# Keeping the outputs of layer 0's last two experts on chip, with the gates applied by slot

## The chip, the cores and the metric

The kernel runs on one core of a Trainium2 chip. The metric is the device time of one execution in microseconds (us). Three executions of the kernel before gave 885.44, 887.4 and 891.0 us, a median of 887.4. TensorE is called PE, VectorE DVE, ScalarE ACT, GpSimd POOL and SyncE SP. Each engine takes its instructions in a fixed order, and each of SP, ACT and POOL also issues DMAs from that same order.

## The reference

The reference is a two-layer transformer block over 256 tokens and 256 context tokens of width 1024. In each layer the two streams pass a modulated RMS norm, three kinds of attention and an output product; then each token is routed to two of 16 experts:

```python
w = w / jnp.sum(w, axis=-1, keepdims=True)
gates = jnp.sum(jax.nn.one_hot(expert_idx, N_EXPERTS) * w[..., None], axis=1)
for e in range(N_EXPERTS):
    hid = jax.nn.silu(t @ w_gate[e]) * (t @ w_up[e])
    out = out + gates[:, e:e + 1] * (hid @ w_down[e])
...
x = x + g2 * moe_ffn(hx, ...)
```

All is float32. Layer 0 routes all 512 tokens, that is four tiles of 128 (two of the context, two of x). Layer 1 needs only x, and its experts run in another way ("paired"), which the change touches in names alone.

## The kernel before, in words

A float32 product is made of three: each operand is split into a rounded part and the rest (`whi`, `wlo` of a weight; `xh`, `xl` or `Xh`, `Xl` of the tokens), and `mm3` issues hi by hi, lo by hi, hi by lo. ACT casts the hi part (L234), DVE subtracts for the lo part (L235).

**Layer 0's routing, then its experts.** `Route.lists` (L1840 and on) ends the routing. One-hot rows `ohs` (slot by token, for the first and the second choice) times token numbers gave `ips`, from which `idx` says for each expert which token stands in each of its 128 slots. `rows` says for each token in which row of the table `yrows` its two expert outputs will stand, and `gates` with what weights. `experts` then loops over 16 experts: an indirect DMA gathers an expert's tokens from `h2row` (`xg`); PE transposes them; ACT and DVE split them; `first` makes gate and up products from split weights (`produce` splits one half of a weight at a time, up to LEAD ahead); `hidden`, `turn` and `second` make y, the expert's output by slot. `write` copies y from PSUM on ACT (L211) and writes it by a DMA from ACT's queue to `yrows` in DRAM (L1095). All this is issued in the order in which it is written (`manual_schedule`).

**The seam between the layers** is `next_in`, also in written order. `combine` issues eight indirect gathers on POOL (L1393): per tile of tokens two, `yc`, one for each choice. `sum_pairs` has the steps of a tile: `one` (ACT: first choice times gate, L1405), `both` (DVE: plus second choice times gate, L1408), `times` (by g2, L1411, on DVE for tile 0 and on POOL for the others), `add` (into the tokens, L1414). `tokens_in` has the norm and the modulation: `square` (ACT, L226), `root` (DVE `ms` and POOL `rstd`, L219 and L221), `scale` (`xn`, DVE, L655), `turn` (eight PE transposes, L193), `modulate` (`xf`, four pieces on ACT, L686, and four on DVE, L684), `high` (`Xh`, ACT, L690) and `low` (`Xl`, DVE, L694). `half(t, h)` then issues 12 products 128x512 of tile t with half of the weight columns `w_in` (L205 to L207). In a turn of the loop PE gets the transposes of tile t-1, `half(t-2, 1)` and `half(t-1, 0)`.

A `Ring` hands out places for weights on their way in, and issues the next load when a place is given back.

## Time and profile before

| | |
|---|---|
| median of three executions | 887.4 us |
| profiled execution | 888.22 us, of which the span of instructions 886.3 |
| mean granted TensorE clock | 0.95 of 2.4 GHz |
| PE busy | 784.3 us (88% of the span) |
| DVE busy | 582.4 us (66%) |
| ACT busy | 447.6 us (50%) |
| POOL busy | 222.2 us (25%) |
| chain that ended last | PE 66%, DVE 16%, DMA 8%, ACT 3%, issue 3%, POOL 2% |

Matmuls are pipelined, so an entry's duration is longer than the spacing of two in a row; where a rate matters, the starts of the first and the last of a row are compared. The granted clock has two levels, 1.2 and 2.4 GHz, printed as 0.50 and 1.00; a window that holds both shows a mean of them. The loop of the experts runs from about 342 to 500 us, the seam from 500 to 553.

### The profile page before, as it was taken

How to read it: one execution, taken by the hardware profiler on the slowest of the kernel's cores; microseconds unless marked ns; L12 is line 12 of the kernel's file. 1: busy time of each engine (PE TensorE's matmuls, PEld its weight loads, DVE VectorE, ACT ScalarE, POOL GpSimd, SP SyncE). 2: the span in 40 equal slices, each digit the busy share in tenths (PEclk: the TensorE clock that was granted, in tenths of full speed). 3: DMA queues.
4: the chain of work that ended last, by engine and by line, in shares of the span. 5: the costliest groups of instructions: out<-in, count | busy, mean ns of one | idle time of the engine just before them, and what ended most of it. 6: DMA issues, size and time to landing. Idle time of an engine off the chain costs nothing.

```text
span 886.3 us, 12972 instructions
## 1 busy us (share of the span) xinstructions
PE 784.3 (88%) x4731; PEld 576.3 (65%) x4731; DVE 582.4 (66%) x1200; ACT 447.6 (50%) x861; POOL 222.2 (25%) x258
## 2 busy tenths in 40 slices
PE   4899999889989977999999549998899797999984
PEld 0578878445557746999999438887555565656541
DVE  1577673879863798899999586697667566221226
ACT  2454442667773416888888546462466543111112
POOL 2000101556320133443342472100423101000200
PEclk9999999999999988999999859999899997999987
DMA  9952221667879337899993757342188955999981
GB/s 319 344 185 96 95 96 48 247 270 284 275 214 376 121 148 263 306 388 401 400 408 156 249 195 292 128 158 95 51 331 215 340 186 215 350 423 422 419 333 51
DMA packets 54505, 219.18 MB, mean 247 GB/s; under 512 B 10299, under 2 KB 10299, under 8 KB 36640
## 3 DMA queue, kind: packets, MB, share of 16 engines
q1 hardware_dynamic: 40816, 182.34, 55.0%
q0 software_dynamic: 8736, 24.92, 7.9%
q10 hardware_dynamic: 4880, 11.00, 3.2%
q8 instruction: 39, 0.64, 0.3%
q14 instruction: 34, 0.28, 0.1%
HBM read 207.09 MB, written 16.84 MB: 253 GB/s over the span
## 4 chain that ended last, share of the span: by engine, by line
PE 66%; DVE 16%; DMA 8%; ACT 3%; issue 3%; POOL 2%; SPq 0%; ACTq 0%; POOLq 0%; DVEq 0%
PE mm L207 7%; PE mm L206 7%; PE mm L205 7%; PE tp L193 6%; PE gu L1189 6%; PE ada L459 4%; PE gu L207 4%; PE gu L205 3%; PE gu L206 3%; DMA wraw<-in_w_up 3%; PE sc L1466 3%; PE w L1245 3%; DVE wlo L235 2%; PE w L1154 2%; DVE nm L1480 2%
## 5 line engine op out<-in xcount | busy, mean ns | idle before, releaser
L235 DVE TENSOR_TENSOR wlo<-wraw,whi 128x1024 fp32r<-128x1024 f32 x136 | 186.1, 1392 | 43.0 <-ACT whi L234 40.5
L234 ACT CAST whi<-wraw 128x1024 fp32r<-128x1024 f32 x152 | 152.8, 1050 | 57.7 <-PE mm L207 35.5
L205 PE MATMUL mm<-whi,Xh 128*128 128x512 f32 x288 | 116.3, 405 | 5.1 <-ACT Xh L690 4.7
L206 PE MATMUL mm<-wlo,Xh 128*128 128x512 f32 x288 | 115.3, 400 | 0.5 <-DVE wlo L235 0.5
L207 PE MATMUL mm<-whi,Xl 128*128 128x512 f32 x288 | 115.0, 399 | 0.5 <-DVE Xl L694 0.5
L221 POOL TENSOR_TENSOR rstd<-ms,cst 128x1 f32<-128x1 f32 (+2 forms) x34 | 29.4, 864 | 272.1 <-DVE ms L219 263.2
L1493 ACT ACTIVATE e<-sc,nm 128x512 f32<-128x512 f32 (+1 forms) x96 | 58.4, 613 | 42.4 <-DVE nm L1486 22.6
L207 PE MATMUL gu<-whi,xl 128*128 128x256 f32 x256 | 74.3, 290 | 0.0
L205 PE MATMUL gu<-whi,xh 128*128 128x256 f32 x256 | 74.2, 290 | 0.0
L206 PE MATMUL gu<-wlo,xh 128*128 128x256 f32 x256 | 72.7, 284 | 0.0
L1189 PE MATMUL gu<-wraw,xq 128*64 128x256 f32 x512 | 64.4, 396 | 3.7 <-DMA wraw<-in_w_up 3.7
L205 PEld LDWEIGHTS mm<-whi,Xh 128*128 128x128 f32 x288 | 55.1, 191 | 18.7 <-ACT Xh L690 6.2
L207 PEld LDWEIGHTS mm<-whi,Xl 128*128 128x128 f32 x288 | 55.0, 191 | 13.9 <-DVE Xl L694 1.5
L206 PEld LDWEIGHTS mm<-wlo,Xh 128*128 128x128 f32 x288 | 55.1, 191 | 12.8 <-DVE wlo L235 1.2
L235 POOL TENSOR_TENSOR wlo<-wraw,whi 128x1024 fp32r<-128x1024 f32 x16 | 42.7, 2672 | 81.1 <-ACT whi L234 50.3
L1189 PEld LDWEIGHTS gu<-wraw,xq 128*64 128x64 f32 x512 | 37.9, 142 | 24.1 <-DMA wraw<-in_w_up 4.2
L193 PEld LDWEIGHTS tp<-ident,e 128*128 128x128 f32 x240 | 26.1, 142 | 40.8 <-issue 21.1
L1480 DVE TENSOR_REDUCE nm<-sc 128x1 f32<-128x512 f32 x64 | 41.2, 684 | 16.5 <-PE sc L1466 11.6
L207 PEld LDWEIGHTS gu<-whi,xl 128*128 128x128 f32 x256 | 49.3, 193 | 1.1 <-DVE xl L1050 0.4
L205 PEld LDWEIGHTS gu<-whi,xh 128*128 128x128 f32 x256 | 49.6, 194 | 0.3 <-ACT xh L1049 0.3
L206 PEld LDWEIGHTS gu<-wlo,xh 128*128 128x128 f32 x256 | 49.5, 193 | 0.0
L193 PE MATMUL tp<-ident,e 128*128 128x128 f32 x240 | 37.8, 286 | 8.4 <-DVE e L1534 3.9
(348 smaller groups left out, 1625.4 us busy)
## 6 DMA issues: line engine op xcount, KB each, us to landing
wraw<-in_w_ada SPq DMA_DIRECT2D x40, 1024.0 KB, 4.9
wraw<-in_w_gate SPq DMA_DIRECT2D x32, 1024.0 KB, 10.1
wraw<-in_w_up SPq DMA_DIRECT2D x32, 1024.0 KB, 11.0
wraw<-in_w_down SPq DMA_DIRECT2D x32, 1024.0 KB, 14.1
wraw<-in_w_in SPq DMA_DIRECT2D x14, 1024.0 KB, 5.2
wraw<-in_w_ada SPq DMA_DIRECT2D x16, 512.0 KB, 8.1
yrows<-y ACTq DMA_DIRECT2D x16, 512.0 KB, 8.1
wraw<-in_w_in POOLq DMA_DIRECT2D x5, 1024.0 KB, 11.9
```

Source lines behind the costliest of these rows:

```text
L193: self.nc.tensor.transpose(out, in_, self.k["ident"][:n, :n])
L205: mm(out, lhsT=xh, rhs=wh, start=start, stop=False)
L206: mm(out, lhsT=xh, rhs=wl, start=False, stop=False)
L207: mm(out, lhsT=xl, rhs=wh, start=False, stop=stop)
L221: nc.gpsimd.tensor_tensor(r, ms, self.k["mhalf"][:, :width], OP.pow)
L234: nc.scalar.copy(h, raw[:, lo:hi])
L235: (engine or nc.vector).tensor_tensor(l, raw[:, lo:hi], h.bitcast(F32), OP.subtract)
L459: nc.tensor.matmul(ps[32 * j:32 * j + 32, :], lhsT=self.silu_c[:, kc, :], rhs=raw[:, 512 * j:512 * j + 512], start=kc == 0, stop=kc == NKC ...
L1189: nc.tensor.matmul(gu[PSLOTS * g:PSLOTS * g + PSLOTS, 256 * b:256 * b + 256], lhsT=xq[q][:, kc, c:c + PSLOTS], rhs=raw[:, kc * 256:kc * 25 ...
L1245: nc.tensor.matmul(y[hf][gs], lhsT=hT[:, c, 0:PSLOTS] if p == NP else hT[:, c, gs], rhs=raw[:, c * D + o * 512:c * D + o * 512 + 512], sta ...
L1480: V.reduce_max(self.nm[:, i:i + 1], self.ps[i], axis=AX.X)
L1493: nc.scalar.activation(self.e[i][:, :self.nkey], self.ps[i], AF.Exp, scale=0.125, bias=self.nm[:, i:i + 1], accum_out=self.z[i])
```

## The change

The outputs of experts 14 and 15 (`LATE_E = 2`) of layer 0 are not written to DRAM. They stay on chip as `ylate`, already times their gates, split in two parts by ACT and DVE. Per tile, products with one-hots `turned` (slot by token, 128x128 for each tile and each of the two experts) take them to their tokens: 32 products 128x512 into PSUM. A token whose choice is expert 14 or 15 gathers a row of zeros instead: the gathers read 14 experts' rows plus one row, which is zeroed at the start of the kernel. So the gathers no longer depend on the last two experts.

The gate is applied where y is copied from PSUM, by slot. For that, `weigh` (in the routing) makes the normalised weights, splits them into three float16 parts, and eight small products with `ohs` bring them to the slots. `one` is gone; `both` is a plain sum; `plus` adds the PSUM banks of the late products. In the seam `times` is always on DVE, all eight pieces of `modulate` are on ACT, and `square(t)` comes behind both halves. Two of the four `w_in` splits, and the place for the ring `rawD`, come later. The bank `ada` of layer 1's projection becomes a fourth `tp` bank.

```diff
-PS_IN = dict(mm=4, ada=1, tp=3)
+PS_IN = (dict(mm=4, ada=1, tp=3), dict(mm=4, tp=4))
...
+            if self.late(0):
+                zeros = self.per.tile([128, 512], F32, tag="modrow", name="zeros")[:, :NKC]
+                nc.gpsimd.memset(zeros, 0.0)
+                z = (NEXP - self.late(0)) * SLOTS
+                nc.gpsimd.dma_start(self.yrows[z:z + 1, :].rearrange("o (p k) -> (o p) k", k=NKC), zeros)
...
-        def modulate(h):
+        def modulate(h, act=False):
...
-                    if b % 2:
+                    if b % 2 and not act:
                         nc.vector.tensor_scalar(xf[b][:, c], tv[:, c], mul, add, OP.mult, OP.add)
                     else:
                         nc.scalar.activation(xf[b][:, c], tv[:, c], AF.Identity, scale=mul, bias=add)
...
-            for name, t in (("one", 0), ("both", 0), ("times", 0), ("one", 1), ("add", 0)):
-                step(sums, t, name)
+            for k in range(self.late(l - 1)):
+                for t in range(2):
+                    step(sums, t, "late", k)
+            for name in ("both", "plus", "times", "add"):
+                step(sums, 0, name)
+            for k in range(self.late(l - 1)):
+                step(sums, 2, "late", k)
             step(ins, 0, "square")
             step(sums, 1, "both")
             step(ins, 0, "root")
-            step(sums, 1, "times", self.nc.gpsimd)
-            step(sums, 2, "one")
+            step(sums, 1, "plus")
             for t in range(1, 6):
                 step(ins, t - 1, "scale")
-                step(sums, t + 1, "both")
-                step(sums, t + 1, "times", self.nc.gpsimd)
-                step(sums, t, "add")
+                if t == 1:
+                    parts.extend(next(split) for _ in range(2))
                 for h in range(2):
                     step(ins, t - 1, "turn", h)
-                    step(ins, t - 1, "modulate", h)
+                    step(ins, t - 1, "modulate", h, True)
+                    step(ins, t - 1, "high", h)
                 half(t - 2, 1)
-                step(ins, t - 1, "high", 0)
-                step(ins, t - 1, "high", 1)
+                step(sums, t, "times")
+                step(sums, t, "add")
                 step(ins, t, "square")
-                step(sums, t + 2, "one")
                 step(ins, t - 1, "low", 0)
+                step(ins, t - 1, "low", 1)
+                if t == 1:
+                    parts.extend(split)
+                    for k in range(self.late(l - 1)):
+                        step(sums, 3, "late", k)
+                    self.ring.open(self.rawD, "rawD", RAW["D"], 2)
+                step(sums, t + 1, "both")
                 step(ins, t, "root")
+                step(sums, t + 1, "plus")
                 if t == 1:
                     self.ring.until(2, self.nc.gpsimd)
-                step(ins, t - 1, "low", 1)
                 half(t - 1, 0)
...
-            w[u] = self.split(t, s * 1024, s * 1024 + 1024, nc.gpsimd if name == "w_down" and s else None)
+            w[u] = self.split(t, s * 1024, s * 1024 + 1024, nc.gpsimd if name == "w_down" and s and n < N - 1 else None)
...
+            if k >= 0:
+                y = self.rawD.tile([128, 2, D], F32R, tag=f"rawD{k}", name="ylate")
...
+                    nc.scalar.activation(y[:, 0, o], ys[n][hf], AF.Copy, scale=gate)
+                    nc.vector.scalar_tensor_tensor(y[:, 1, o], ys[n][hf], gate, y[:, 0, o].bitcast(F32), OP.mult,
+                                                   OP.subtract)
+                return
+            y = mo.tile([128, D], F32, tag="y", name="y", bufs=2)
...
-                self.copy(y[:, hf * 512:hf * 512 + 512], ys[n][hf], True)
+                nc.scalar.activation(y[:, hf * 512:hf * 512 + 512], ys[n][hf], AF.Copy, scale=gate)
...
-            nc.vector.scalar_tensor_tensor(y0, y1, self.gates[:, 1, i:i + 1], y0, OP.mult, OP.add)
+            nc.vector.tensor_tensor(y0, y0, y1, OP.add)
+
+        def late(k):
+            if k == 0:
+                bs.extend(self.bank("tp") for _ in range(2))
+            for hf in range(2):
+                for part in range(2):
+                    nc.tensor.matmul(bs[hf], lhsT=self.turned[k][:, i * 128:i * 128 + 128],
+                                     rhs=self.ylate[k][:, part, hf * 512:hf * 512 + 512],
+                                     start=k == part == 0, stop=part == 1 and k == len(self.ylate) - 1)
+
+        def plus():
+            for hf, b in enumerate(bs):
+                o = slice(hf * 512, hf * 512 + 512)
+                nc.vector.tensor_tensor(y0[:, o], y0[:, o], b, OP.add)
...
+            if ps == 0:
+                self.weigh()
+            gate = m.rt.tile([128, 16], F32, tag=f"gate{ps}", name="gate")
+            for i in range(T):
+                for w in range(2):
+                    self.nc.tensor.matmul(ips[:, 64:112], lhsT=self.ohs[i][:, w],
+                                          rhs=self.gv[:, w, i].rearrange("p a e -> p (a e)"),
+                                          start=i == w == 0, stop=i == T - 1 and w == 1)
...
+        for k in range(late):
+            m.turned.append(m.per.tile([128, 512], F32R, tag=("modrow", "brow")[k], name="turned"))
+            for i in range(T):
+                V.tensor_scalar(m.turned[k][:, i * 128:i * 128 + 128], cst[:, C_IOTA:C_IOTA + 128],
+                                own[:, i, k:k + 1], None, OP.is_equal)
```

What this does to the order on the engines, at three places. First DVE at the end of layer 0's routing, before the change (`wlo` is the first expert's weights, `xl` its tokens):

```order
L1854 TENSOR_SCALAR idx<-ips 128x16
L1860 TENSOR_TENSOR picke<-oh,cst 128x128
L1866 TENSOR_TENSOR pickg<-oh,score 128x128
L1862 TENSOR_REDUCE e<-picke 128x8
L1867 TENSOR_REDUCE gates<-pickg 128x8
L1863 SCALAR_TENSOR_TENSOR rows<-e,first 128x8
L1868 TENSOR_TENSOR gsum<-gates 128x4
L1869 RECIPROCAL gsum<-gsum 128x4
L1870 TENSOR_TENSOR gates<-gates,gsum 128x8
L235 TENSOR_TENSOR wlo<-wraw,whi 128x1024 x4
L1050 TENSOR_TENSOR xl<-tp,xh 128x512 x2
```

DVE at the same place after the change, from the row that now comes ahead of `idx`; these eight rows hold nine operations up to the first part of `gv`:

```order
L1945 TENSOR_TENSOR pickg<-oh,score 128x128
L1906 TENSOR_SCALAR idx<-ips 128x16
L1946 TENSOR_REDUCE g<-pickg 128x8
L1947 TENSOR_TENSOR g<-g 128x4
L1948 RECIPROCAL g<-g 128x4
L1949 TENSOR_SCALAR g<-g 128x4
L1951 TENSOR_TENSOR pickg<-pickg,g 128x64 x2
L1952 CAST gv<-pickg 128x8x16
```

The weights are now made first, to be split. DVE again, five small operations further on, from `gate`, which takes the result of PE's small products, to the first expert's tokens:

```order
L1915 TENSOR_REDUCE gate<-ips 128x16
L1923 SCALAR_TENSOR_TENSOR e<-e,pos 128x8
L1928 TENSOR_SCALAR g<-ips 128x2
L1916 TENSOR_SCALAR gate<-gate 128x16
L1924 TENSOR_SCALAR rows<-e 128x8
L1928 TENSOR_SCALAR g<-ips 128x2 x3
L1932 TENSOR_SCALAR turned<-cst,g 128x128 x8
L239 TENSOR_TENSOR wlo<-wraw,whi 128x1024 x4
L1076 TENSOR_TENSOR xl<-tp,xh 128x512 x2
```

In all, 22 small operations (`idx` among them) and eight one-hots 128x128 now stand ahead of the first `wlo`, where there were nine small ones from `idx` on.

Second, DVE in the seam, before the change, from the last `wlo` to the first tile's `Xl`:

```order
L235 TENSOR_TENSOR wlo<-wraw,whi 128x1024 x4
L1408 SCALAR_TENSOR_TENSOR yc<-yc,gates 128x1024
L1411 TENSOR_TENSOR yc<-yc,wraw 128x1024
L1414 TENSOR_TENSOR xc<-xc,yc 128x1024
L1408 SCALAR_TENSOR_TENSOR yc<-yc,gates 128x1024
L219 TENSOR_SCALAR ms<-nss 128x1
L655 TENSOR_SCALAR xn<-xc,rstd 128x1024
L1408 SCALAR_TENSOR_TENSOR yc<-yc,gates 128x1024
L1414 TENSOR_TENSOR xc<-xc,yc 128x1024
L684 TENSOR_SCALAR xf<-tp,sc_2522,sh_2521 128x128 x4
L694 TENSOR_TENSOR Xl<-xf,Xh 128x4x128
```

And after it, to the first `Xl` again:

```order
L1125 SCALAR_TENSOR_TENSOR ylate<-y,gate,ylate 128x512 x4
L1443 TENSOR_TENSOR yc<-yc 128x1024
L1457 TENSOR_TENSOR yc<-yc,tp 128x512 x2
L1460 TENSOR_TENSOR yc<-yc,wraw 128x1024
L1463 TENSOR_TENSOR xc<-xc,yc 128x1024
L1443 TENSOR_TENSOR yc<-yc 128x1024
L223 TENSOR_SCALAR ms<-nss 128x1
L1457 TENSOR_TENSOR yc<-yc,tp 128x512 x2
L671 TENSOR_SCALAR xn<-xc,rstd 128x1024
L239 TENSOR_TENSOR wlo<-wraw,whi 128x1024 x2
L1460 TENSOR_TENSOR yc<-yc,wraw 128x1024
L1463 TENSOR_TENSOR xc<-xc,yc 128x1024
L710 TENSOR_TENSOR Xl<-xf,Xh 128x4x128 x2
```

The first tile's sum no longer follows `wlo`; the sum takes `plus` from PSUM (`yc<-yc,tp`), `times` (`yc<-yc,wraw`) of each tile is now here, and the pieces `xf` have left.

Third, ACT in the seam, before the change, from the last y copy to the second tile's square:

```order
L211 COPY y<-y 128x512 x2
L1095 DMA yrows<-y 128x1024
L156 DMA wraw<-in_w_in 128x4x512
L234 CAST whi<-wraw 128x1024 x4
L1405 ACTIVATE yc<-yc,gates 128x1024 x2
L226 ACTIVATE xn,nss<-xc 128x1024
L1405 ACTIVATE yc<-yc,gates 128x1024
L686 ACTIVATE xf<-tp,sh_2521,sc_2522 128x128 x4
L690 CAST Xh<-xf 128x4x128 x2
L226 ACTIVATE xn,nss<-xc 128x1024
```

And after it:

```order
L1124 ACTIVATE ylate<-y,gate 128x512 x4
L230 ACTIVATE xn,nss<-xc 128x1024
L238 CAST whi<-wraw 128x1024 x2
L702 ACTIVATE xf<-tp,sh_2524,sc_2525 128x128 x4
L706 CAST Xh<-xf 128x4x128
L702 ACTIVATE xf<-tp,sh_2524,sc_2525 128x128 x4
L706 CAST Xh<-xf 128x4x128
L230 ACTIVATE xn,nss<-xc 128x1024
```

The last DMA to `yrows` and the products by gate are gone; eight pieces `xf` and both `Xh` of a tile now stand between one tile's square and the next one's.

## Rows read from the trace of the kernel before

**Rows 1.** Windows view, core 0: busy us (instructions) per engine, TensorE clock, DMA share, GB/s.

```profile
352.00:499.00 147.00, 146.05 (x1045) 136.47 (x1044) 134.20 (x131) 125.84 (x176) 59.62 (x27) 1.00 0.86 336
```

**Rows 2.** Timeline of DVE, 334 to 343 us: start, duration, instruction [idle before <-releaser].

```profile
333.97 0.48 DVE L1836 TENSOR_SCALAR ohs<-cst,pos 128x128 f16<-128x128 f32 x2
...
334.83 0.28 DVE L1860 TENSOR_TENSOR picke<-oh,cst 128x128 f32<-128x128 f32 x1
...
336.47 4.63 DVE L235 TENSOR_TENSOR wlo<-wraw,whi 128x1024 fp32r<-128x1024 f32 x4
341.56 1.50 DVE L1050 TENSOR_TENSOR xl<-tp,xh 128x512 fp32r<-128x512 f32 x2 [0.46 <-ACT xh L1049]
```

**Rows 3.** Timeline of PE, the same stretch.

```profile
334.31 0.39 PE L1837 MATMUL ips<-val,ohs 128*128 128x16 f16 x2 [0.71 <-DVE ohs L1836]
334.55 3.61 PE L352 MATMUL tp<-mask,ones 128*128 128x256 bf16 x20
340.17 1.55 PE L193 MATMUL tp<-ident,xg 128*128 128x128 f32 x8 [2.00 <-DMA xg<-h2row,idx]
...
342.31 0.58 PE L207 MATMUL gu<-whi,xl 128*128 128x256 f32 x1
```

**Rows 4.** Timeline of PE, layer 0's last y product to the fourth tile of layer 1.

```profile
500.01 0.39 PE L207 MATMUL y<-whi,hl 128*128 128x512 f32 x1
520.51 1.97 PE L193 MATMUL tp<-ident,xn 128*128 128x128 f32 x8 [20.12 <-DVE xn L655]
523.88 0.79 PE L205 MATMUL mm<-whi,Xh 128*128 128x512 f32 x1 [1.40 <-ACT Xh L690]
...
530.04 1.87 PE L193 MATMUL tp<-ident,xn 128*128 128x128 f32 x8
...
537.22 1.03 PE L193 MATMUL tp<-ident,xn 128*128 128x128 f32 x8
...
543.62 1.09 PE L193 MATMUL tp<-ident,xn 128*128 128x128 f32 x8
```

**Rows 5.** Windows view of the seam between the layers.

```profile
526.00:532.00 6.00, 6.00 (x20) 4.88 (x20) 3.69 (x5) 1.68 (x4) 5.96 (x7) 0.52 0.52 164
553.00:573.00 20.00, 19.97 (x92) 16.30 (x91) 14.27 (x38) 8.93 (x21) 2.23 (x2) 1.00 0.28 106
```

**Rows 6.** Timeline of ACT, the end of layer 0.

```profile
488.98 0.33 ACTq L1095 DMA_DIRECT2D yrows<-y  x1
```

**Rows 7.** Timeline of POOL, the same stretch and on.

```profile
491.53 5.99 POOL L235 TENSOR_TENSOR wlo<-wraw,whi 128x1024 fp32r<-128x1024 f32 x2 [7.09 <-ACT whi L234]
504.95 1.00 POOL L1393 DMA_INDIRECT yc<-yrows,rows  x1 [7.43 <-DMA yrows<-y]
...
515.50 0.99 POOL L1393 DMA_INDIRECT yc<-yrows,rows  x1 [0.30 <-issue]
```

**Rows 8.** DMA view, 486 to 540 us: queue, count, KB, median us from issue to landing.

```profile
yrows<-y ACTq DMA_DIRECT2D x3, 512.0 KB, 5.4
...
yc<-yrows,rows POOLq DMA_INDIRECT x8, 5.5
```

**Rows 9.** Timeline of DVE in the seam.

```profile
511.76 1.28 DVE L1408 SCALAR_TENSOR_TENSOR yc<-yc,gates 128x1024 f32<-128x1024 f32 x1 [0.79 <-DMA yc<-yrows,rows]
...
517.62 2.83 DVE L655 TENSOR_SCALAR xn<-xc,rstd 128x1024 f32<-128x1024 f32 x1 [0.69 <-POOL rstd L221]
```

**Rows 10.** Timeline of ACT in the seam.

```profile
515.59 1.06 ACT L226 ACTIVATE xn<-xc 128x1024 f32<-128x1024 f32 x1 [1.54 <-DVE xc L1414]
...
521.67 1.51 ACT L686 ACTIVATE xf<-tp,sh,sc 128x128 f32<-128x128 f32 x4 [3.89 <-PE tp L193]
523.21 0.62 ACT L690 CAST Xh<-xf 128x512 fp32r<-128x512 f32 x1
```

**Rows 11.** Lines of 500 to 552.9 us by form: busy us, mean ns | idle before it.

```profile
L221 POOL TENSOR_TENSOR rstd<-ms,cst 128x1 f32<-128x1 f32 x4 | 3.2, 808 | 9.1 <-DVE ms L219 9.1
...
L655 DVE TENSOR_SCALAR xn<-x,rstd 128x1024 f32<-128x1024 f32 x2 | 1.5, 754 | 0.9 <-POOL rstd L221 0.9
```

90 lines of the change are left out of this document (58 added, 32 removed).

## The prediction

> **What bounds the kernel now.** I began with the shares of busy time by engine and the chain that ended last: PE is on two thirds of that chain, so what counts is where PE stands still or slow. The windows show where it doesn't. In the loop of layer 0's experts PE is busy 146.05 of 147 us at full clock [rows 1], and behind the seam 19.97 of 20 us [rows 5]. In such a stretch a late start is not caught up and an early one is not lost. So the change is worth what it shifts at the two places where PE waits: the start of the loop, and the seam between the layers. PE's timeline and its waits show both: ahead of the loop 2.00 us for the first gather [rows 3], and in the seam 20.12 us until DVE's `xn` lets the first tile's transposes go [rows 4]. The reader is to follow that `xn` back: the sum of tile 0 waits for gathered rows [rows 9], the first gather waited 7.43 us for the last experts' rows to land in DRAM [rows 7], and these could be written only behind the last y product at 500.01 [rows 4].
>
> **The start of the loop (loses).** `wlo` of the first expert now stands behind 22 small DVE operations and eight one-hots, where nine small ones stood. In the old order the eight small ones from `picke` to `wlo` took 336.47 - 334.83 = 1.64 us, 0.2 us each [rows 2]. The new ones up to the split weights `gv` number twelve, at 0.2 us each 2.4 us, from about 334.7 to 337.1. Then PE makes eight small products; two like them took 0.39 us [rows 3], so eight take some 1.5 us, to 338.6. DVE has three operations to do meanwhile, then `gate` and eight small ones wait for PE. These are mostly independent of each other, and I take 0.08 us each, 0.6 in all, since small independent ones overlap (an estimate; at 0.2 it is 1.6). The eight `turned` follow: two `ohs` of the same size took 0.48 us [rows 2], so eight take 1.9. They end at 341.1, and the four `wlo` (4.63 us [rows 2]) at 345.7. Then comes `xl`, 0.75 us for the first half, half of 1.50 [rows 2]. The first product that needs it, at 342.31 before [rows 3], goes at 346.4: **+4.1 us**. The gather of the first tokens, which PE waited for until 340.17 [rows 3], does not hide this: it was ready while DVE was still in `wlo`, and `wlo` with `xl` behind it is last in both orders. PE's 20 warming products (3.61 us [rows 3]) now stand behind the small ones and end near 342, still ahead of `xl`. ACT's casts no longer wait for DVE's `pickg`, which gains nothing. Bounds: if the small ones overlap throughout and `turned` are faster, +2.5; if each costs 0.2 and PE's clock needs longer to come back, +5.6. PE has no slack in the 147 us that follow, so it reaches the seam in full.
>
> **The loop itself (nothing).** The y copy with a gate is the same ACT pass. Two y buffers in place of three: a write lands 5.4 us after its issue [rows 8], within an expert's period (147 us are some 15 experts, 9.8 us each). The last expert's second `wlo` moves from POOL to DVE, one pass of 1.16 us (4.63/4) [rows 2], where PE has products queued. The zeroing of one row lies at the kernel's start on POOL and under the first weight loads; its cover is the wait for those loads, and without it it would cost about one POOL issue, 1 us [rows 7].
>
> **The seam (gains, then gives back).** All on the clock of before; the +4.1 comes on top.
> - *Gathers.* The first one now waits for expert 13's write, issued at 488.98 [rows 6], 5.4 us to landing [rows 8]: 494.4. POOL's `wlo`, two in 5.99 us from 491.53 [rows 7], had its first done by about 494.5. So the gathers go from 494.7 and not from 504.95 [rows 7]; with 1.3 us between issues and 5.5 us to landing [rows 8], tile 0's pair is there at 502 to 503.
> - *Late outputs.* The last y product ends at 500.4 [rows 4]. Two ACT and two DVE passes of 128x512 follow, alternating, 0.62 us each by the `Xh` row [rows 10]: done at 502.4. PE has done expert 14's products by then and needs 1 us for tile 0's last four (128x512 products go at 0.23 us each: 24 of them and 8 transposes lie between 537.22 and 543.62 [rows 4]).
> - *Tile 0.* `both` 502.8 to 504.0 (1.2, a 128x1024 pass as `wlo`), `plus` two halves 1.4, `times` 1.2, `add` 1.2: 507.8. `square` 1.06 [rows 10] with its small ends, to 509.2; `rstd` 0.81 and `xn` 0.75 [rows 11], no longer 2.83 beside POOL's `times` [rows 9]: **transposes at 511**, not 520.51 [rows 4], **9.5 us earlier**.
> - *First product.* Ahead of it PE has tile 3's eight late products, which need banks that come free when all eight `xf` are done: 0.5 + 1.5 + 0.62 + 1.5 us [rows 10] from 512, then 1.8 to 3.4 us for the eight, so about 518; before 523.88 [rows 4]. **Six earlier.**
> - *Tiles 1 to 3.* The period of a tile was PE's work, 543.62 - 537.22 = 6.40 us [rows 4]. Now one chain runs in series from a tile's transposes to the next one's: half the transposes 0.6, four `xf` 1.5, `Xh` 0.62, four `xf` 1.5, `Xh` 0.62 [rows 10], `square` 1.06 and its small ends 0.5, `rstd` 0.81, `xn` 0.75 [rows 11] = about **8 us**. Before, DVE took half of the `xf` at the same time, and the chain stayed under PE's work. The second tile's transposes come at about 523.5 (12 products from 518 at half clock), not 530.04; the third's at 532, not 537.22; the fourth's at 540.5, not 543.62 [rows 4]. Behind the seam PE has no slack [rows 5], so what stands there stays: **-3 us**.
>
> All 32 late products cost 32 x 0.23 = 7.4 us of PE, nearly all in the old gap of 20.12 us; without that cover they would cost just that. Bounds of the seam: -7 if the chain overlaps better than its sum, +5 if the clock stays low (below).
>
> **Sum.** 888.22 + 4.1 - 3 = 889.3 for the profiled execution, which lies 0.8 above the median of the runs shown; against that median 888.5. I say **889**.
>
> **The clock, row against rule.** Before, PE is idle from 500.4 to 520.5 [rows 4] and the clock granted in 526 to 532 is 0.52, so nearly all of that window at 1.2 GHz; it is back at 1.00 from 532 on [rows 5], some 8 us behind the first dense product. I take the same here: half clock up to the second tile, then full. The Trainium skill, "TensorE: Matmul & The Clock Gate", section "HAM oscillation — how this bites in real kernels", says that PE work in bursts with waits between can be throttled again and again, each burst starting cold. No row here shows whether gaps of under 2 us in an 8 us period do that. By the rule the clock would stay low through the tiles, which is the second rival.
>
> **The rivals.**
> 1. *The lead is kept* (chance 0.12). If `xf` and `Xh` of a tile's halves overlap with the transposes and the period stays near 6.4, the 9.5 us come through to 6 or all, and if the start costs only 2.5: 888.2 - 9.5 + 2.5 = 881, at worst 888.2 - 6 + 2.5 = 885. For it: DVE's `xn` at 2.83 [rows 9] was slow beside POOL and POOL is now quiet. Against it: the chain's rows sum to 8 us, and ACT is one engine.
> 2. *The clock stays at 1.2 GHz through the tiles* (0.14; ends slower). PE waits about 1.6 us in each 8 us period. At half clock a tile is 24 x 0.43 + 1.9 = 12.2 us (12 products in about 5.2 of the 6.16 us between 523.88 and 530.04, which hold a wait; transposes 1.87 [rows 4]). Then the tiles start at 523.5, 535.7 and 547.9, the last 4.3 later than 543.62: 888.2 + 4.1 + 4.3 = 896.6. It decides if the second tile's products still run low. For it: low clock was the state there before, until 532 [rows 5]. Against it: PE is denser before the tiles than it was, since 32 late products stand in the old gap.
> 3. *The gathers don't come earlier* (0.12): POOL issues them while DVE is busy 134 of 147 us [rows 1], and the rows land no sooner than the 511.76 at which the first sum could go before [rows 9]. Then the transposes are at 520, and the slower period takes 4.8 us by the fourth tile: 888.2 + 4.1 + 4.8 = 897. For it: POOL's own pass slowed DVE's `xn` from 0.75 to 2.83 [rows 9, 11], so the two do disturb each other. Against it: the old gathers also went beside DVE passes and landed in 5.5 us [rows 8]. The Trainium skill, "SBUF — State Buffer", section "Who interferes with whom", says that a DMA issued from POOL can be starved while DVE holds the port that they share. By that page this rival is how it goes; the trace of before bears it out only so far that one pass was slowed, and no gather landed late there.
>
> **How the numbers follow.** The forecast, a small loss or gain, has 0.62, its own range 885 to 893 by the bounds of the two terms. Rival 1 reaches to 880, rivals 2 and 3 to 898. With a tenth left out on each side the range is 880 to 897. A measurement of this kernel tells 1%, 8.9 us, from no change. Faster by more than that, under 878.5, needs the whole lead and a hidden start: 0.1, more than rival 1 alone gives, for gains in the seam that the rows don't show. Slower, over 896.3: half of rivals 2 and 3 and a little of the forecast, 0.15. Within 1%: 0.75.
>
> **What would show it.** First `xl` product near 346.4; gathers from about 499 (494.7 + 4.1); first transposes of layer 1 at about 515; spacing of the four tiles' transposes about 8 us with PE waiting for `xn` each time; clock 1.00 from about 536. The forecast is wrong if the spacing is 6.4 (rival 1), if clock 0.50 lasts beyond 540 (rival 2), if the first gathered pair lands behind 512 (rival 3), or if the time moved at a place not named here, as in layer 1's weight loads.

## The result, and the profile after

The change took **895.95 us** (median of five runs, 894.08 to 896.15) against 887.4 for the kernel before: a ratio of 1.0083, 95% interval 1.0056 to 1.0110. It is slower by 0.8%, within 1% by these runs, though the interval reaches past 1% and e9 (the same kernel again, below) came out at 1.0129. It lies 7 us above the forecast of 889. The profiled execution took 895.97 us, 7.75 more than that of before. The engines and the chain that ended last, on the page of the profile after (its span is 894.1 us):

```profile
PE 799.9 (89%) x4771; PEld 585.6 (65%) x4771; DVE 589.3 (66%) x1220; ACT 451.1 (50%) x873; POOL 206.2 (23%) x256
PE 65%; DVE 17%; DMA 6%; ACT 5%; issue 3%; POOL 2%; ACTq 0%; SPq 0%; DVEq 0%; POOLq 0%
```

The shares say almost nothing: POOL works 16.0 us less than before, PE 15.6, DVE 6.9 and ACT 3.5 us more. So I cut both traces at PE rows that stand in both kernels and compared the stretches between. Times are us between the starts of two PE rows. The last column is e9, the changed kernel run once more without any edit, which tells what repeats.

| stretch, from one PE row to the next | before | after | differs by | e9 |
|---|---|---|---|---|
| layer 0: first scores of attention to early output products (not changed) | 120.62 | 123.02 | +2.40 | 120.32 |
| on to routing's first `ips` (not changed) | 59.06 | 58.89 | -0.17 | 59.10 |
| `ips` to the first product with `xl` | 8.00 | 13.02 | **+5.02** | 13.00 |
| on to the second expert's first such product | 9.11 | 9.85 | +0.74 | 9.86 |
| on to the last gate and up product | 141.72 | 142.12 | +0.40 | 142.10 |
| on to the last y product | 6.87 | 10.11 | **+3.24** | 10.86 |
| on to the first tile's transposes of `xn` | 20.50 | 10.24 | **-10.26** | 10.48 |
| on to the fourth tile's | 23.11 | 29.97 | **+6.86** | 29.55 |
| on to the scores of layer 1's attention | 82.27 | 84.20 | **+1.93** | 84.23 |
| on to the end | 246.69 | 244.40 | -2.29 | 243.43 |

The first and the last row nearly cancel. The first does not repeat in e9; 1.8 of the last row's 2.29 lie in layer 1's output product, which takes about 27.3 or 28.9 us from run to run and took 29.07 before. What repeats is the middle: start +6.2 (three rows), the loop's end +3.2, the seam -3.4, layer 1's projection +1.9.

**The start.** PE's timeline and DVE's, at the same place as [rows 3] and [rows 2]. Columns: start, duration, instruction [idle before it <- releaser].

```profile
339.51 0.48 PE L1912 MATMUL ips<-gv,ohs 128*128 128x48 f16 x8 [2.71 <-DVE gv L1955]
343.72 1.04 PE L197 MATMUL tp<-ident,xg 128*128 128x128 f32 x8
349.42 0.38 PE L211 MATMUL gu<-whi,xl 128*128 128x256 f32 x1 [3.64 <-DVE xl L1076]
```

```profile
339.16 0.29 DVE L1955 TENSOR_TENSOR gv<-picke,gv 128x128 f16<-128x128 f32 x1
...
340.64 3.56 DVE L1932 TENSOR_SCALAR turned<-cst,g 128x128 fp32r<-128x128 f32 x8
344.12 4.64 DVE L239 TENSOR_TENSOR wlo<-wraw,whi 128x1024 fp32r<-128x1024 f32 x4
348.69 1.27 DVE L1076 TENSOR_TENSOR xl<-tp,xh 128x512 fp32r<-128x512 f32 x2
```

DVE goes without a pause from one row to the next, and PE waits 3.64 us for what DVE makes last, the `xl` behind the four `wlo`. That is the forecast's picture. The eight `turned` took 3.56 us, though, 0.445 each and not 0.24. Ahead of them PE's eight small products took 0.48 us, where I had put down 1.5, and DVE's twelve operations up to `gv` 2.8 instead of 2.4.

**The loop's end and the seam.** DVE, then PE (as [rows 4]).

```profile
496.37 2.34 DVE L239 TENSOR_TENSOR wlo<-wraw,whi 128x1024 fp32r<-128x1024 f32 x2
...
500.83 3.84 DVE L239 TENSOR_TENSOR wlo<-wraw,whi 128x1024 fp32r<-128x1024 f32 x2 [0.65 <-ACT whi L238]
504.60 0.41 DVE L1094 TENSOR_TENSOR hid<-hid,gu 128x256 f32<-128x256 f32 x1
506.01 0.42 DVE L1104 TENSOR_TENSOR hl<-hT,hh 128x256 fp32r<-128x256 f32 x1 [1.01 <-ACT hh L1103]
506.60 1.41 DVE L1125 SCALAR_TENSOR_TENSOR ylate<-y,gate,ylate 128x512 fp32r<-128x512 f32 x2 [0.17 <-ACT ylate L1124]
```

```profile
505.06 0.51 PE L197 MATMUL hT<-ident,hid 128*128 128x128 f32 x2 [0.64 <-DVE hid L1094]
507.41 0.80 PE L209 MATMUL y<-whi,hh 128*128 128x512 f32 x1 [1.84 <-DVE ylate L1125]
...
511.50 0.39 PE L211 MATMUL y<-whi,hl 128*128 128x512 f32 x1
511.73 5.89 PE L1450 MATMUL tp<-ylate,turned 128*128 128x512 f32 x24
521.74 1.97 PE L197 MATMUL tp<-ident,xn 128*128 128x128 f32 x8 [4.12 <-DVE xn L671]
...
526.51 2.93 PE L1450 MATMUL tp<-ylate,turned 128*128 128x512 f32 x6 [0.84 <-ACT xf L702]
529.24 0.63 PE L209 MATMUL mm<-whi,Xh 128*128 128x512 f32 x1
...
534.73 1.10 PE L197 MATMUL tp<-ident,xn 128*128 128x128 f32 x8 [1.68 <-DVE xn L671]
...
543.62 1.09 PE L197 MATMUL tp<-ident,xn 128*128 128x128 f32 x8 [2.17 <-DVE xn L671]
```

The wait of 20.12 us is gone: 5.89 us of it are late products, 4.12 still a wait. In its place there are waits of 1.68 and 2.17 us ahead of the second and third tile, both for `xn`, where [rows 4] have none. And ahead of the last twelve y products PE waits 0.64 us for `hid`, which stands behind two `wlo` on DVE, and 1.84 us for expert 14's `ylate`, which holds the PSUM banks that these products need. The two `wlo` are slow there: 3.84 us beside POOL's `wlo` (499.99 to 502.46, below), where the pair from 496.37 took 2.34.

The clock, in the windows view (busy us per engine with instructions, then granted clock, DMA share, GB/s):

```profile
508.00:513.00 5.00, 5.00 (x18) 4.01 (x17) 1.04 (x3) 1.37 (x2) 2.28 (x3) 0.74 0.98 383
522.00:531.00 9.00, 7.42 (x21) 5.33 (x21) 7.48 (x8) 7.09 (x14) 0.53 (x1) 0.50 0.17 62
531.00:544.00 13.00, 9.14 (x45) 6.99 (x44) 10.97 (x16) 5.21 (x12) 4.99 (x7) 1.00 0.99 361
544.00:548.00 4.00, 4.00 (x16) 3.30 (x15) 2.61 (x3) 3.63 (x10) 0.00 (x0) 0.59 1.03 389
534.73:543.62 8.89, 6.71 (x33) 5.28 (x33) 6.90 (x10) 5.21 (x12) 3.03 (x5) 1.00 0.98 350
543.62:551.71 8.09, 8.09 (x33) 6.57 (x34) 4.59 (x6) 5.21 (x12) 0.55 (x1) 0.79 1.03 385
```

PE ran at half clock behind three of its waits, and at full clock behind the one of 1.68 us. The last two rows are the periods of the second and the third tile, from transposes to transposes. In the first of them PE is busy 6.71 of 8.89 us and waits for `xn`. In the other it doesn't wait at all: it is busy for all of the 8.09 us, at a mean clock of 0.79.

POOL's timeline shows the gathers ([rows 7]), the DMA view their median from issue to landing ([rows 8]), for all eight and then for the first alone:

```profile
499.99 2.47 POOL L239 TENSOR_TENSOR wlo<-wraw,whi 128x1024 fp32r<-128x1024 f32 x1 [7.29 <-issue]
503.34 1.08 POOL L1431 DMA_INDIRECT yc<-yrows,rows  x1 [0.88 <-PE y L211]
```

```profile
yc<-yrows,rows POOLq DMA_INDIRECT x8, 5.8
...
yc<-yrows,rows POOLq DMA_INDIRECT x1, 7.2
```

The trace has the landing of three of the eight, the first and the last two, so 5.8 speaks for the last ones. The first took 7.2 us. ACT's load of `w_in` (1 MB) went out at 502.49, 0.85 us ahead of it.

**Layer 1's projection.** PE is dense at clock 1.00 there in both kernels, yet slower now. These are two products of the same kind with 39 product steps between their starts before, and 36 after:

```profile
565.90 0.39 PE L206 MATMUL mm<-wlo,Xh 128*128 128x512 f32 x1
...
574.75 0.39 PE L206 MATMUL mm<-wlo,Xh 128*128 128x512 f32 x1
```

```profile
574.25 0.39 PE L210 MATMUL mm<-wlo,Xh 128*128 128x512 f32 x1
...
582.67 0.40 PE L210 MATMUL mm<-wlo,Xh 128*128 128x512 f32 x1
```

8.85 / 39 = 0.2269 us a product before, 8.42 / 36 = 0.2339 after. Over the whole projection the means are 0.2278 and 0.2342. For the 324 products of this kind from the fourth tile's transposes to the scores that makes 324 x 0.0064 = 2.1 us, about the +1.93 of the table.

### The profile page after: what moved, and what is told of

The parts are those of the page before. It is cut to its first block, busy times and chain, and to the rows that moved or that the text cites. A ratio compares the mean times of both kernels' runs of the same rounds, so it can differ in the third digit from the quotient of the medians.

```text
span 894.1 us, 13073 instructions
## 1 busy us (share of the span) xinstructions
PE 799.9 (89%) x4771; PEld 585.6 (65%) x4771; DVE 589.3 (66%) x1220; ACT 451.1 (50%) x873; POOL 206.2 (23%) x256
## 4 chain that ended last, share of the span: by engine, by line
PE 65%; DVE 17%; DMA 6%; ACT 5%; issue 3%; POOL 2%; ACTq 0%; SPq 0%; DVEq 0%; POOLq 0%
PE mm L210 7%; PE mm L211 7%; PE mm L209 7%; PE tp L197 6%; PE gu L1227 5%; PE ada L472 4%; PE gu L211 4%; PE gu L209 3%; PE gu L210 3%; PE sc L1515 3%; PE w L1283 3%; DVE wlo L239 3%; DMA wraw<-in_w_up 2%; PE w L1192 2%; PE poB L1689 2%
## 5 line engine op out<-in xcount | busy, mean ns | idle before, releaser
L239 POOL TENSOR_TENSOR wlo<-wraw,whi 128x1024 fp32r<-128x1024 f32 x15 | 37.0, 2464 | 84.0 <-ACT whi L238 44.7
```

Source lines behind the costliest of these rows:

```text
L239: (engine or nc.vector).tensor_tensor(l, raw[:, lo:hi], h.bitcast(F32), OP.subtract)
```

## Experiments

Every run stands beside runs of the kernel before on the same chip; ratios are to those. The base of all edits is the changed kernel. Its own two ratios, 1.0083 above and 1.0129 in e9, differ by as much as most of the effects below, so I go by stretches above all.

**e1: the one-hots later.** `turned` is built from the loop of the experts, one piece in each expert from the fourth on.

```diff
-            for i in range(T):
-                V.tensor_scalar(m.turned[k][:, i * 128:i * 128 + 128], ...)
+                    if n > 2:
+                        next(one_hots, None)
```

> The eight one-hots `turned` are built in the loop, one after each expert from the fourth on, from the token numbers in `idx`, and not ahead of the first expert. Theory (a late start in front of a dense PE is not caught up): the first product with `xl` goes about 4 us earlier than in the changed kernel (its `turned` took 3.56 us there, and four small ones go too), and the time falls by 4 to 4.5, to about 891.5 us. Rival (the start is hidden or given back later, by weight loads in the loop or in layer 1): the first product goes 4 us earlier, but the time falls by less than 1.5, to 894.5 or more.

Measured: 892.71 us, ratio 1.0052 [1.0031, 1.0074]. From `ips` to the first `xl` product 9.32 us instead of 13.02; DVE's `wlo` now starts 339.06:

```profile
339.06 4.63 DVE L239 TENSOR_TENSOR wlo<-wraw,whi 128x1024 fp32r<-128x1024 f32 x4
```

The 3.7 us are those of the eight `turned`. The half clock behind PE's wait goes too (8.39 for the next stretch, 9.85 before this edit), and 1.7 come back in the rest of the loop, where the pieces now stand (143.84 us instead of 142.12). By the ratios about 2.8 us are left, though the two intervals overlap. So the start's loss is `turned`, for the most part.

**e2: half of the modulation back on DVE.**

```diff
-                    step(ins, t - 1, "modulate", h, True)
+                    step(ins, t - 1, "modulate", h)
```

> `modulate` gives half of the pieces `xf` back to DVE, the order of the steps stays as in the changed kernel. Theory (the tile's period of 8.1 to 8.9 us is the ACT chain alone): each period falls by about 1.4 us (one group of four `xf` goes beside the other), towards PE's 6.4; three periods give 4 us, time about 892. Rival (DVE, which now also has `times` for each tile, is as full: `xn` 0.75, `xf` 1.35, `times` 1.22, `add` 1.22, two `Xl` 1.38, `both` 1.22, `plus` 1.28 make 8.4 us a tile): the period stays within 0.5 us of the changed kernel's, time 895 to 897.

Measured: 898.17 us, 1.0124 [1.0095, 1.0153]. The spacings of the tiles' transposes are 13.61, 10.14 and 8.00 us against 12.99, 8.89 and 8.09. The theory fails, since no period falls by 1.4 us. The rival is nearer, but not shown: the second spacing grew by 1.25 us and not by less than 0.5, and PE is busy for 9.44 us of it at a clock of 0.71, so half clock has a part in it. Nor is DVE full: it is busy 8.05 of 10.15 us in the second and 5.84 of 8.00 in the third. What its timeline shows is that DVE's four `xf` (1.37 us) now stand ahead of the next tile's `times` and `add`, for which `square` and `xn` wait. So the series is no shorter than with all eight on ACT.

**e3: the next tile's sum and square between the halves.** This shortens the chain by letting `square` go ahead of a tile's second `xf`.

```diff
                 for h in range(2):
+                    if h == 0:
+                        step(ins, t - 2, "low", 1)
+                        step(sums, t, "times")
+                        step(sums, t, "add")
+                        step(ins, t, "square")
```

> Only the order in the seam is changed: `times`, `add` and `square` of the next tile come behind the first half's `Xh`, ahead of the second half's `xf`; the second half's `Xl` moves behind the next tile's `xn`. Theory (one series of steps from a tile's transposes to the next one's sets the period, the engines are not full): the chain loses one `xf` group and one `Xh`, 2.1 us; DVE's own work of 7.2 us is then the period, so it falls from 8.1 to 8.9 to about 7.2 to 7.5, three periods give 3 to 4 us, time about 892.5. Rival (the period is the clock of PE, half of the seam's products being at 1.2 GHz): spacing stays over 8 us, time 895 to 896.5.

Measured: 897.26 us, 1.0110 [1.0079, 1.0141]. PE's rows of the seam:

```profile
528.11 2.93 PE L1451 MATMUL tp<-ylate,turned 128*128 128x512 f32 x6 [3.30 <-ACT xf L702]
535.30 1.09 PE L197 MATMUL tp<-ident,xn 128*128 128x128 f32 x8 [0.22 <-DVE xn L671]
542.12 1.09 PE L197 MATMUL tp<-ident,xn 128*128 128x128 f32 x8
```

The spacings are 14.42, 6.82 and 6.56: with the chain cut, the period falls to PE's own 6.40 of [rows 4], and the waits for `xn` are 0.22 us and none. That is the chain theory; the clock is 1.00 in both periods. The first spacing grows, because tile 3's late products stand in front of PE and wait 3.30 us for the later `xf`. The total is no better, since two stretches with no edit in them were longer (85.76 to the scores, 77.72 on to the output product; 84.20 and 75.65 after).

**e4: the last expert.** The copies of expert 14's y ahead of expert 15's `hid`, and its last `wlo` back on POOL.

```diff
-            w[u] = self.split(..., nc.gpsimd if name == "w_down" and s and n < N - 1 else None)
+            w[u] = self.split(..., nc.gpsimd if name == "w_down" and s else None)
+                if n == N:
+                    write(n - 2)
```

> At the end of the loop expert 14's `ylate` is made ahead of expert 15's transposes, and the last expert's second `wlo` goes back to POOL. Theory (PE's late end of the loop, 11.4 us behind the kernel before where it was 8.2 behind at 485 us, comes from those two: `hid` waits 0.8 behind a second `wlo` on DVE, the last products wait 1.0 for DVE's `ylate`, and the pause puts the clock down, 1.2): the last y product comes 2 to 3 us earlier and so does the first `xn`, time about 893.5. Rival (the first `xn` waits for gathered rows or something else than the last y product; with `wlo` back on POOL the gathers start 2.5 us later): last y product earlier, `xn` not, time 895.5 to 898.

Measured: 897.49 us, 1.0126 [1.0084, 1.0168]. From the last gate and up product to the last y product 7.12 us instead of 10.11: the 3 us of the loop's end are these two things and the clock behind the waits, which stays at 1.00 here. e5 and e7 below tell the two apart. Then the gathers are behind POOL's `wlo`, and DVE's first sum waits for them:

```profile
496.13 5.79 POOL L239 TENSOR_TENSOR wlo<-wraw,whi 128x1024 fp32r<-128x1024 f32 x2 [7.27 <-ACT whi L238]
502.08 1.00 POOL L1433 DMA_INDIRECT yc<-yrows,rows  x1 [0.15 <-issue]
```

```profile
508.74 1.23 DVE L1445 TENSOR_TENSOR yc<-yc 128x1024 f32<-128x1024 f32 x1 [2.16 <-DMA yc<-yrows,rows]
```

So 12.49 us pass to the first transposes instead of 10.24. The early write is right, the `wlo` on POOL is not: it takes the gathers' place.

**e5: gates by slot alone.** No late experts.

```diff
-LATE_E = 2
+LATE_E = 0
```

> The changed kernel with no late experts (`LATE_E = 0`): gates by slot, the new order of the seam, but all 16 outputs go to DRAM and the gathers wait for the last ones again; no `turned`, no late products. Theory (the start loses by `gv` and `turned`, the seam gains at the first transposes and loses by the period): the first `xl` product comes 3.5 to 4 us earlier than in the changed kernel, as without `turned`; the end of the loop has the old pace; the first transposes come some 20 us behind the last y product, not 10.2, with a period near 8 us still: about 888 + 2 (start) + 6 (period) = 896, as slow as the changed kernel. Rival (late experts are what costs): the time comes near the kernel before, under 890.

Measured: 899.64 us, 1.0141 [1.0118, 1.0165]. The expected time was 896. The start falls to 9.30 (no `turned`). The loop's end falls to 7.86: with `wlo` on DVE but no `ylate` it is 1.0 above the 6.87 of before, PE waits 0.63 us for `hid`, and the clock stays at 1.00. PE waits 18.32 us for the first `xn`, as before the change. The period stays near 9 and 7.6 us. So by the stretches the late experts do pay for themselves: without them the seam's new order costs its 6 us (29.10 us from the first tile to the fourth, 23.11 before), and only 1.8 are gained ahead of it.

**e7: all of it at once.** One-hots later, the early write, the square early, tile 3's late products in two accumulator banks ahead of the transposes, and two `w_in` splits on POOL.

```diff
+                        if t == 1:
+                            engine.append(self.nc.gpsimd)
+                            parts.append(next(split))
```

> Four edits of the changed kernel together. `turned` is made in the loop. Expert 14's `ylate` is made ahead of expert 15's transposes. The late products of tile 3 go to two `mm` banks ahead of the first transposes, not between them and the first product. The seam's order is: second half's `Xl`, `plus`, `times`, `add` and `square` of the next tile ahead of the second `xf` group, `xn` ahead of `plus`; the second two `w_in` splits on POOL. Theory (each of the named waits is worth its own size in front of a dense PE): start 4 to 4.8 earlier, last y product another 2, first transposes as before 10.2 behind it, the fourth's some 22 to 24 us behind the first's (not 30): 895.9 - 4.4 - 2 - 6.5 = 883. Rival (the shares don't add, since layer 1's weight loads or the clock take the lead back): 888 or more.

Measured: 888.89 us, 1.0021 [1.0000, 1.0041]. Start, loop's end and seam are shorter (9.71, 7.49 and 27.32 us), not as much as expected (a time of 883, and 22 to 24 us for the seam): beside POOL's `wlo` (2.58 and 2.37 us, from 521.05 on) two of DVE's passes were held.

```profile
521.34 2.83 DVE L710 TENSOR_TENSOR Xl<-xf,Xh 128x512 fp32r<-128x512 f32 x1
...
525.83 2.87 DVE L671 TENSOR_SCALAR xn<-xc,rstd 128x1024 f32<-128x1024 f32 x1 [0.46 <-POOL rstd L225]
```

Elsewhere they take 0.69 and 0.75. The loop's end of 7.49 has `wlo` still on DVE, and PE's wait of 0.64 us for `hid` with it; what went is the wait for `ylate` and the half clock behind it, 2.6 us.

And DVE's first sum waited 1.86 us for gathered rows, so that 12.20 us passed to the first transposes. The first two gathers took 7.9 us to landing. That is not new: the first one took 7.2 in the changed kernel, and the first five 7.7 (median) in e9. In all three ACT's load of `w_in` goes out some 0.9 us ahead of the first gather. The later end of the loop had hidden it. e10 puts the load behind the last `ylate`.

**e8: the edits of the seam alone**, those of e7 without start and loop's end.

> The seam's edits alone (tile 3's late products ahead of the first transposes, the new order, the second two splits on POOL), start and end of the loop as in the changed kernel. Theory (the period and the first product are set by the series of steps in this order): from the first tile's transposes to the fourth's 22 to 24 us, not 30; time about 889.5. Rival (the tiles are paced by the half clock of PE and not by the order): the stretch stays over 28 us, time over 894.

Measured: 895.25 us, 1.0093 [1.0058, 1.0128]; 27.32 us from the first tile to the fourth instead of 29.97, and the same two held passes. Expected were 22 to 24 us, and the ratio does not show the 2.6 us.

**e9: the changed kernel again**, unaltered.

> The changed kernel once more, unaltered, for a second profile. Theory (the 2.4 us that its first profile lost in layer 0's attention and output product, where no line is changed, came from the clock granted in that execution): this profile takes 120.4 to 121.5 us from the first score product to the eleventh output product, not 123.0, and the stretches around the start, the loop's end and the seam repeat to 0.2 us. Rival (something in the change, such as the zeroed row or a moved tile, makes that stretch slower each time): 123 us again.

Measured: 896.88 us, 1.0129 [1.0083, 1.0174]; four runs from 893.44 to 900.49. The stretches of the table repeat within 1 us, but for layer 0's attention, 2.7 us shorter. (Expected was 0.2 us: the loop's end is 0.75 longer here, since all twelve last y products ran at half clock.) There the windows view of after reads

```profile
255.00:275.00 20.00, 15.73 (x76) 10.50 (x77) 9.16 (x17) 10.99 (x20) 4.26 (x7) 0.83 0.63 219
```

and that of e9, a window 1.0 us earlier,

```profile
254.00:274.00 20.00, 15.21 (x96) 10.88 (x95) 11.20 (x24) 12.84 (x24) 4.26 (x7) 1.00 0.51 185
```

The same program met the clock at 0.83 once and at 1.00 once: some 2 us that come and go without any edit.

**e10: without POOL's splits.** As e7, but all splits on DVE, `plus` ahead of `xn` from the third tile on, and ACT's `w_in` load behind the last `ylate`.

```diff
-            with self.tc.issue_after(self.written.ins):
+            with self.tc.issue_after(self.last.ins):
...
+                if t > 1:
+                    step(ins, t - 1, "low", 0)
+                    step(sums, t + 1, "both")
+                    step(ins, t, "root")
+                    step(sums, t + 1, "plus")
```

> The four edits together once more (`turned` in the loop, `ylate` of expert 14 early, tile 3's late products ahead, the seam's order), with three differences. All `w_in` splits are on DVE, the second pair around tile 1's `xn` (on POOL they held DVE's `Xl` and `xn` for 2.8 us each, which take 0.7 alone). From tile 2 on `plus` stands ahead of `xn` again, as in the run with the early square, whose periods were 6.8 and 6.6 us and not 8.1 and 7.3. And the `w_in` load on ACT's queue comes behind the last `ylate`, so that the first gathers (7.9 us to landing beside it, 5.4 without) come through sooner. Theory (each wait is worth its size): fourth transposes 24.5 to 25.5 us behind the first ones, not 27.3; first ones 10.2 to 11 behind the last y product, not 12.2; time 884 to 886, below the kernel before (887.0 to 887.4). Rival (the seam's lead is lost behind it, since ACT is then 98% busy, or the gathers are late for another reason): 888 or more.

Measured: 889.78 us, 1.0016 [1.0002, 1.0030], twelve runs. The stretches came as expected: 10.25 us to the first transposes, 25.23 on to the fourth. The first two gathers, now ahead of the load, landed 4.5 and 5.4 us behind their issue, those issued behind it after 8.0 to 8.7, and no sum waited for them. PE's transposes in the seam:

```profile
515.73 1.09 PE L197 MATMUL tp<-ident,xn 128*128 128x128 f32 x8 [2.28 <-DVE xn L671]
...
540.96 1.03 PE L197 MATMUL tp<-ident,xn 128*128 128x128 f32 x8
```

The time did not: 11.2 us were gained from `ips` to the fourth tile, and the end came 6.4 earlier. One place where it went: 85.79 us on to the scores instead of 84.20. The windows view of the 16 us from 56 us behind the fourth tile, after and then e10:

```profile
607.70:623.70 16.00, 13.98 (x69) 11.13 (x68) 13.74 (x27) 4.51 (x8) 1.24 (x1) 1.00 0.25 82
```

```profile
597.00:613.00 16.00, 13.98 (x63) 10.97 (x61) 13.18 (x27) 3.59 (x6) 1.21 (x1) 0.89 0.22 70
```

The same busy time and the same wait (2.02 us for `qBC` in both), but behind it 0.89 of clock: 2 x 0.11 x 16 = 3.5 us at half clock, so some 1.7 us lost. The kernel before waited 2.46 us at the same place and kept 1.00.

**e11 and e12: 32 bytes.** For the spacing in layer 1's projection: a pad of 32 bytes in the pool from which that stage takes its split weights `whi` and `wlo`, in the changed kernel (e11) and in e10 (e12). It is meant to move these weights. `Xh` and `Xl` come from another pool. The traces hold no addresses, so the move itself is not shown.

```diff
+            self.nc.gpsimd.memset(self.wsp.tile([128, 8], F32, name="pad"), 0.0)
```

> The changed kernel with one unused tile of 32 bytes a partition in the pool of layer 1's projection, so that the split weights there begin 32 bytes lower: at a multiple of 64 bytes, as in the kernel before, and not 32 beyond one. Theory (in layer 1's projection the 128x512 products of the changed kernel start 0.234 us apart, in all its variants, where before it was 0.2275 at the same granted clock, since the weights lie at another place): the spacing goes back to 0.2275 to 0.230, the stretch from the fourth tile's transposes to the first scores from 84.2 to about 82.5 us, the time falls by 2 to 3, to about 893. Rival (the spacing comes from something else, as the banks or what runs beside): it stays at 0.234, time 894.5 to 897.

> The best seam so far (`turned` in the loop, expert 14's `ylate` early, late products ahead, new order) with the same 32 bytes. Theory: as there, 2 to 3 us less than without them: 886.5 to 888, the kernel before being at 887 to 888. Rival: the spacing stays at 0.234 and the time at 889 to 890.

Measured: e11 897.21 us, 1.0094 [1.0071, 1.0117], spacing 0.2328 (mean over the projection) where 0.2342 stood and 0.2275 was expected. The pad takes away 0.0014, not 0.007; that much is no chance, since all runs without it have 0.2341 to 0.2343 and the three with it 0.2325 to 0.2328. e12 887.52 us, 0.9994 [0.9977, 1.0010], spacing 0.2325. This time is the one that the theory named, but by luck: the spacing did not fall as it says, and what it did fall is worth some 0.5 us.

**e13: three transpose banks.** e12 with layer 1's accumulators back in PSUM banks 3 to 6, where they lay before the change; the fourth `tp` bank had pushed them to 4 to 7.

```diff
-PS_IN = (dict(mm=4, ada=1, tp=3), dict(mm=4, tp=4))
+PS_IN = (dict(mm=4, ada=1, tp=3), dict(mm=4, tp=3))
...
-                    step(sums, t, "late", k)
+                    step(sums, t, "late", k, ("tp", "mm")[t])
```

> The run before this one (edits of the start, the end and the seam together, and the layer's inputs 32 bytes further on), with layer one's transpose banks back to three, so that its accumulators lie in PSUM banks 3 to 6 as in the kernel before and not in 4 to 7; of the four late tiles the second and the fourth then take their late products into accumulator banks. Theory (the spacing of the 128x512 products of layer one's projection, 0.2275 us before and 0.233 to 0.234 in every variant since, hangs on the banks): the spacing comes back to 0.2275 to 0.229, the stretch from the fourth tile's transposes to the next attention's scores is 2 to 2.5 us shorter (85.5 to about 83), and the time is 885 to 886. Up to 1 us may be lost at the first tile, whose second half of transposes finds one bank fewer. Rival (the banks have no part in it): the spacing stays at 0.233 and the time at 887 to 889.

Measured: 887.44 us, 0.9990 [0.9975, 1.0006], twelve runs. PE's rows of the projection, 42 product steps apart:

```profile
564.07 0.40 PE L210 MATMUL mm<-wlo,Xh 128*128 128x512 f32 x1
...
573.83 0.40 PE L210 MATMUL mm<-wlo,Xh 128*128 128x512 f32 x1
```

9.76 / 42 = 0.2324 (mean 0.2327): the rival holds, the banks have no part in it. The stretch to the scores is 85.51 us, with the clock at 0.89 behind a wait of 2.18 us for `qBC`, as in e10. What the fourth bank is worth shows too: with three the first two tiles' second transposes wait 1.60 us for `xf`, and nothing is lost, 25.21 us to the fourth tile against 25.23 in e10.

## Why the prediction was right or wrong

- **The number.** 895.95 lies in the stated range of 880 to 897, but 2.95 beyond the 885 to 893 that the forecast itself had. The upper end of the range was there for rivals 2 and 3, and neither is what made the time. So the range held in part by luck, while the loss within 1% is what was forecast.
- **The start: right in kind, mis-sized.** +4.1 forecast, +5.0 measured to the first `xl` product, and +6.2 up to the loop's last gate and up product, beyond the bound of +5.6. (The product went at 349.42 and not at 346.4; 2.1 us of that were late already at routing's `ips`.) The term that was off is `turned`: eight at 0.24 us were taken from `ohs`, which writes f16; these write fp32r and took 0.445, so 3.56 us instead of 1.9 (e1 gives 3.7 back). PE's eight small products, 0.48 us and not 1.5, took some of that away. The longer wait of PE costs clock as well, which the forecast had in its bound and not in its sum: 0.74 more by the second expert.
- **"The loop itself (nothing)": wrong, +3.2.** This is the step that failed, in two parts. The smaller one is `wlo`. The step said of the last expert's second `wlo` that it moves to DVE, one pass of 1.16 us, "where PE has products queued". PE had twelve y products queued, and they ended first: `hid` stood behind two `wlo` that took 3.84 us beside POOL's own. That alone costs 1.0 us in e5 and 0.6 in e7 and e10. The larger part the step did not see: `ylate` is a second reader of the y banks, on DVE behind `hid`, where the y copy had been on ACT alone. The last expert's y began 6.02 us behind the last gate and up product and not 4.22, 0.8 us of it by `hid` and 1.0 by the wait for `ylate` (1.84 us, where PE had waited 0.95 for ACT's copy). Behind that wait the twelve products took 4.09 us instead of 2.65, at a clock of 0.74 in 508 to 513. e7 and e10, which at this place only put `ylate` of expert 14 earlier, give 2.6 us back (7.49 and 7.48); e4, with `wlo` on POOL as well, 3.0 (7.12).
- **The seam: right in its sum.** Transposes of tile 0 forecast 11.0 us behind the last y product, measured 10.24; the first product another 7.0 behind, measured 7.50; the first to the fourth tile 29.5 us, measured 29.97. The periods were 8.89 and 8.09 us where 8 was forecast. The first is the chain, with PE waiting for `xn`. The other came out at 8 by another way, PE busy throughout at a clock of 0.79; in e4, where the clock was 1.00 there, it is 7.69 and PE waits 0.97 us for `xn`, so the chain stood close behind. e3 shows the chain's part: with the chain cut, the two are 6.82 and 6.56. Rival 1, a period near 6.4, did not happen in this kernel. The seam's balance is -3.4; -3 was forecast.
- **The clock, row against rule.** Half clock lasted to 531 and then came 1.00, as I had it, but 544 to 548 fell to 0.59 once more, behind the wait of 2.17 us. The Trainium skill, "TensorE: Matmul & The Clock Gate", section "HAM oscillation — how this bites in real kernels", says that bursts with waits between can start cold each time. Its case has longer waits than these. The trace agrees for one of the two waits in the tiles, and not for that of 1.68 us, nor for one of 2.11 in e9, behind which the clock was 1.00. So rival 2, whose tiles all ran at half clock with a period of 12.2 us, is not what happened, but for a part of the third tile, although the time came out near its 896.6.
- **Rival 3: not what set the time, but a part of it happened.** The gathers went at 503.34, 1.95 us behind the last gate and up product; 494.7 on the clock of before was 1.6 behind it. They were not quite free of the last experts: by POOL's timeline the first was released by a y product of expert 14, and the sixth waited 2.34 us for the last one of expert 15. The first landed after 7.2 us and not 5.5, at 510.5, where the forecast had the first pair at about 507. DVE's first sum had to wait for `ylate` until 513.3 in any case, so it cost nothing here; it cost 1.86 us in e7, where the loop ended earlier, and 2.16 in e4, where the gathers also started later. The Trainium skill, "SBUF — State Buffer", section "Who interferes with whom", says that DMAs issued from POOL can be starved by DVE, but also that `tensor_tensor` was not seen to do it. DVE's passes beside the first gathers are of that kind or `scalar_tensor_tensor`, and e10 points at the load on ACT's queue, so this rule was not tested, and the forecast leaned on it too far. The same section says that DVE and POOL passes contend, and that agrees: 2.83 and 2.87 us in e7 beside POOL's `wlo`, 0.69 and 0.75 elsewhere.
- **Not in the forecast: layer 1's projection, +1.9.** It was listed as what would make it wrong, "if the time moved at a place not named here". The cause is open. It is not the clock (1.00) and not the banks (e13), and the 32 bytes in the pool of the split weights (e11) take away about a fifth of it. Not tried: other places of these weights, the places of `Xh` and `Xl`, and what the other engines and the DMAs do beside.
- **The sum.** Of the 7.75 us between the two profiles the forecast has 6.2 - 3.4 = 2.8 where it had 1.1. Another 5.2 are the loop's end and the projection; the unchanged stretches nearly cancel.

No version beat the kernel before: e12 and e13 equal it (0.9994 and 0.9990, both intervals hold 1). In e13, 10.25 us are gained up to the first tile's transposes; 2.4 are lost in the start and the loop, 0.6 at its end, 2.1 in the tiles and 3.2 in the projection.

## What to carry to other kernels

When a step moves to another engine "under queued work", count how long that queue still lasts at exactly that place: in the last turn of a loop there is no next turn to fill it. Count the step at what it takes beside the other engine's pass (here 3.84 us for 2.34). A buffer that gets a second reader comes free when the slower of the two is done, and that reader's place in its engine's queue is part of the price. Price a new elementwise operation by a row with the same output type, not only the same shape, and check gains against stretches that the edit does not touch before believing a median.

## What the runs showed of the hardware

- The mean spacing of 128x512 products at clock 1.00 in layer 1's projection was 0.2278 us before and 0.2325 to 0.2343 in the variants of the kernel, 2.1 us over 324 products. Cause open, as told above.
- A gather issued some 0.9 us behind a load of 1 MB on ACT's queue took 7.2 to 7.9 us to landing (after, e9, e7), and 4.5 with the load behind it (e10). The DMA share was 0.93 in 495 to 509 of e7 and 0.86 in 496 to 510 of e10.
- A 128x128 `tensor_scalar` on DVE took 0.445 us with an fp32r result, 0.24 with f16 [rows 2].
- At the same place PE sometimes kept its clock and sometimes fell to half: 0.83 and 1.00 in two executions of one program, 1.00 and 0.89 behind the same 2.02 us in two kernels, 1.00 behind 2.46 us at that place in the kernel before. Stretches that no edit touched came out at one of two lengths, 8.83 or 10.3 us at the start of layer 0's output product, 37.2 or 38.8 from layer 1's output product to its experts. This is likely what makes the single runs of one kernel differ by several us: e10's fastest run (884.7) had a mean clock of 0.961, its slowest (891.9) 0.954.
